# Half-empty products of a long convolution run in adjacent pairs, with channels turned modulo 8

## The chip, the cores and the metric

The kernel runs on one core of one Trainium2 chip. The metric is the device time of one execution in microseconds (us); less is better. A core has a matrix engine (TensorE, PE in the profile, with its weight loads as PEld), a vector engine (VectorE, DVE), a scalar engine (ScalarE, ACT), a general engine (GpSimd, POOL) and a queue engine (SyncE, SP), which here issues most of the transfers (DMAs). Matrix products read from the core's memory (SBUF, 128 partitions) and write to banks of a second memory (PSUM), from which DVE or ACT must take them away.

## The reference

One encoder layer over 2048 positions with 1024 channels. The input is normalised and projected; a part of the projection passes a width-3 convolution and then two rounds of a long two-sided convolution with gates (the Hyena group, 512 channels), the rest goes through a bidirectional mLSTM. Both are joined, projected and added to the input; cross-attention into 256 memory rows and an MLP follow, then a last normalisation. All is float32. What the change touches:

```python
def _hyena(hy, spec, skip):
    L = hy.shape[1]
    u = hy.astype(jnp.float32)
    z, g1, g2 = u[..., :D_HYENA], u[..., D_HYENA:2 * D_HYENA], u[..., 2 * D_HYENA:]
    for o, gate in enumerate((g1, g2)):
        conv = jnp.fft.irfft(jnp.fft.rfft(z, n=2 * L, axis=1) * spec[:, o], n=2 * L, axis=1)[:, :L]
        z = gate * (conv + z * skip[o].astype(jnp.float32))
    return z
```

`spec` is the spectrum of filters that a small network computes for every position: two sine layers of width 64, an output layer from 64 to 2 x 2 x 512 (two rounds, forward and backward filter), and a decay window.

## The kernel before, in words

The Fourier transforms of length 4096 are done as matrix products in two stages, with the sequence index written as t = 16 q + j (q from 0 to 127, j from 0 to 15). A first stage runs over q for each j: the matrix `f1`, two blocks of 128x128 for even and odd frequencies (`p`). It holds four copies of a 32-point transform, one for each value of q modulo 4; the rest of it is zeros. A second stage mixes j and q modulo 4 with one 128x128 block of `dm` per frequency. The way back has `em` for the second stage and `e2` (two blocks, summed) for the last. A tile of work is 128 partitions by 512 channels, one float32 product that fills one PSUM bank; the profile shows two records for it. The products of the projection and of later layers split their operands in high and low parts instead (`mm3`, lines 336 to 338, three products in a faster format).

The parts that the change touches:

- **`filters`** (205 to 322). For each of 8 steps j2, two rounds o and two j: the output layer gives the forward filter from rows 0 to 63 of the hidden layer (line 286, bank `pf`) and the backward filter from rows 64 to 127 (line 287, bank `pb`). Each is a product that uses 64 of the array's 128 rows. DVE multiplies both by the window (289, 290), DVE and GpSimd form sum and difference (294, 295), and `front` (268) applies `f1` (271), one iteration late. `blocks` (298) then loads the result by frequency and applies `dm` (319).
- **`sweep`** (652) projects 256 channels at a time, channels on partitions, and ends each column tile with the width-3 convolution. **`sweep_out`** (709) brings the tile into natural order: for the 12 tiles of the Hyena group it transposes 16 slices (time modulo 16, 63 or 65 positions each) on TensorE, four to a bank (719), copies each bank out on ACT or DVE in turn (721, `copy` at 171), and stores it with one DMA each (722).
- **`hyena`** (781). `spectrum` (851) applies `f1` to z: for each j two full products (856), copied out by ACT (p = 0) and DVE (p = 1) at 857 and stored at 859, one DMA on ACT's queue and one on SP's. Then 16 steps per round multiply by `dm` (880), by the filter's spectrum (882 to 886) and by `em` (846, in `back`). The last stage (891 to 902) sums two full products with `e2` in one bank (899), and DVE multiplies by the gate (900). In round one that is the next `spectrum`'s input, one iteration late. `load1`, `load2`, `load3` ask for data one or two steps ahead on SP's queue.

Order: `program` (1795) weaves `filters` with the first sweeps, then `hyena` with the remaining ones, by work units that the generators yield. A scheduler with a time model then fixes each engine's order of instructions, in which an engine waits at an instruction until all that it needs is there. PSUM has four banks for the projection (`mm`, 155) and four for the convolution (`hy`, 158), each used in turn. Products of the projection stand on TensorE between those of the convolution.

Of the kernel before, what the change touches and what calls it, by code (L numbers as in the profile page):

```python
# [18 lines left out]
L = 2048  # L19
# [8 lines left out]
def shape_constants():  # L28
# [30 lines left out]
    e2 = f1.transpose(0, 2, 1) * (wgt.reshape(2, 128, 1) / 4096.0)  # L59

# [8 lines left out]
    for par in range(2):  # L69
# [21 lines left out]
        "c_e2": e2.transpose(1, 0, 2),  # L91
# [34 lines left out]
class Prog:  # L126
    def __init__(self, ctx, tc, a):
        self.tc, self.nc, self.a = tc, tc.nc, a
        nc = self.nc
        self.ctx = ctx  # L130
        self.dr = ctx.enter_context(tc.tile_pool(name="dr", bufs=1, space=DRAM))
        self.s = {}
        cp = self.cp = ctx.enter_context(tc.tile_pool(name="cp", bufs=1))
        ident = cp.tile([128, 128], F32, name="ident")
        nc.gpsimd.memset(ident, 1.0)
        nc.gpsimd.affine_select(ident, ident, pattern=[[-1, 128]], compare_op=ALU.is_equal, fill=0.0,
                                base=0, channel_multiplier=1)
# [5 lines left out]
        self.flip = 0  # L143
        self.pending = []
# [13 lines left out]
    def hy(self):  # L158
        return self.ps.tile([128, 512], F32, tag="hy", name="hy", bufs=4)
# [45 lines left out]
    def filters(self):  # L205
# [4 lines left out]
        if True:  # L210
# [66 lines left out]
            for j2 in range(8):  # L277
# [3 lines left out]
                for o in range(2):  # L281
                    st = [ta() for p in range(2)]
                    for jj in range(2):
                        j = 2 * j2 + jj
                        pf, pb = self.hy(), self.hy()
                        nc.tensor.matmul(pf, hid[0:64, j], w3[0:64, o], start=True, stop=True)
                        nc.tensor.matmul(pb, hid[64:128, j], w3[64:128, o], start=True, stop=True)
# [421 lines left out]
    def sweep_out(self, ct, cv, t0, n):  # L709
# [3 lines left out]
        if ct < 12:  # L713
            q0, nq = t0 // 16, n // 16
            dst = self.d_hy[ct // 4].rearrange("(q j) c -> q j c", j=16)[q0:q0 + nq]
            for j4 in range(4):
                pt = self.mm().rearrange("p (k t) -> p k t", k=4)
                for jj in range(4):
                    nc.tensor.transpose(pt[0:nq, jj], cv[:, 4 * j4 + jj:n:16], self.ident)
                st = sb.tile([128, 4, 128], F32, tag="st", name="st", bufs=3)  # L720
                self.copy(st[0:nq], pt[0:nq])
                nc.sync.dma_start(out=dst[:, 4 * j4:4 * j4 + 4, cc], in_=st[0:nq])
            return
# [57 lines left out]
    def hyena(self, es):  # L781
        nc, tc, a = self.nc, self.tc, self.a
        hy = self.dram("hy", (3, L, CH)).rearrange("s (q j) c -> s q j c", j=16)
        hd = self.dram("hd", (2, 32, 128, CH))
        yh = self.dram("yh", (L, CH)).rearrange("(q j) c -> q j c", j=16)
        sds = [self.dram(f"zs{o}", (2, 128, 16, CH)) for o in range(2)]
        gds = [self.dram(f"zg{o}", (2, 128, 16, CH)) for o in range(2)]
# [8 lines left out]
        f1 = sb.tile([128, 2, 128], F32, name="f1")  # L796
        e2 = sb.tile([128, 2, 128], F32, name="e2")
        nc.sync.dma_start(out=f1, in_=a["c_f1"])
        nc.sync.dma_start(out=e2, in_=a["c_e2"])
        ghy = self.bcast(sb, a["hy_norm_g"], CH, "ghy")  # L800
        def load1(j2):
            z = ta()
            js = slice(2 * j2, 2 * j2 + 2)
            nc.sync.dma_start(out=z, in_=hy[0, :, js])
            return z

        def load2(o, i):
            p, k = divmod(2 * i, 16)
# [5 lines left out]
            nc.sync.dma_start(out=t, in_=sds[o][p, 8 * k:8 * k + 16].rearrange("(k r) j c -> (r j) k c", k=2))  # L814
# [29 lines left out]
        def back(m, em, y, gs, dst):  # L844
# [3 lines left out]
            if m == 1:  # L848
                nc.scalar.dma_start(out=dst.rearrange("(k r) j c -> (r j) k c", k=2), in_=gs)

        def spectrum(o, j2, z):
            st = [ta() for p in range(2)]
            for jj in range(2):
                for p in range(2):
                    pp = self.hy()
                    nc.tensor.matmul(pp, f1[:, p], z[:, jj], start=True, stop=True)
                    (nc.vector.tensor_copy if p else nc.scalar.copy)(st[p][:, jj], pp)
            for p in range(2):
                (nc.sync if p else nc.scalar).dma_start(out=sds[o][p, :, 2 * j2:2 * j2 + 2], in_=st[p])
# [7 lines left out]
        for o in range(2):  # L867
            gd = gds[o]
            nxt = load2(o, 0)
            for i in range(16):  # L870
                yield 3.5
                p, k = divmod(2 * i, 16)
# [5 lines left out]
                for m in range(2):  # L878
# [8 lines left out]
                    late(lambda m=m, em=em, y=y, gs=gs, dst=gd[p, 8 * k:8 * k + 16]: back(m, em, y, gs, dst))  # L887
            late(None)
            nxt = load3(o, 0)
            for j2 in range(8):  # L890
# [977 lines left out]
```

## Time and profile before

| | us |
|---|---|
| median of 3 runs | 3330.34 (3326.27 to 3330.63) |
| the profiled execution | 3330.7 |
| its span, first to last instruction | 3329.0 |
| TensorE busy in the span | 3162.2 |
| float32 products of lines 286 and 287, first to last start | 119.6 to 348.5 |
| first stages (line 856), first to last start | 497.4 to 848.8 |
| last stages (line 899), first to last start | 728.9 to 1144.5 |
| transposes of line 719, first to last start | 66.6 to 915.1 |

A row of the profile names line, engine, operation and tiles (`out<-in`), then count, busy time and the mean of one in ns. In rows of TensorE, 64*128 is rows by columns of the array that the product uses. A window row gives its length, then each engine's busy time with the number of instructions, the granted clock, the mean busy share of the 16 DMA engines, and GB/s. TensorE's instructions overlap, so the time that one costs is read from the starts, not from its duration.

### The profile page before, as it was taken

How to read it: one execution, taken by the hardware profiler on the slowest of the kernel's cores; microseconds unless marked ns; L12 is line 12 of the kernel's file. 1: busy time of each engine (PE TensorE's matmuls, PEld its weight loads, DVE VectorE, ACT ScalarE, POOL GpSimd, SP SyncE). 2: the span in 40 equal slices, each digit the busy share in tenths (PEclk: the TensorE clock that was granted, in tenths of full speed). 3: DMA queues.
4: the chain of work that ended last, by engine and by line, in shares of the span. 5: the costliest groups of instructions: out<-in, count | busy, mean ns of one | idle time of the engine just before them, and what ended most of it. 6: DMA issues, size and time to landing. Idle time of an engine off the chain costs nothing.

```text
span 3329.0 us, 45394 instructions
## 1 busy us (share of the span) xinstructions
PE 3162.2 (95%) x15293; PEld 2519.0 (76%) x15293; DVE 1985.2 (60%) x3334; ACT 1512.1 (45%) x2860; POOL 1253.5 (38%) x863
## 2 busy tenths in 40 slices
PE   6999999899999988699999998999999999999998
PEld 5655666667667887598888896888788887888876
DVE  7684324534556656576766564755755576656595
ACT  5442444642564344354454444555655543333335
POOL 0132000220122204634434114876765564434483
PEclk9999999999999999799999999999999999999999
DMA  5554897886787659857557525764754475444434
GB/s 177 177 195 135 284 316 244 241 262 237 217 225 251 211 182 310 262 155 246 172 179 238 191 89 175 229 216 155 222 172 144 161 240 169 127 143 138 130 93 167
DMA packets 472257, 655.70 MB, mean 197 GB/s; under 512 B 39630, under 2 KB 251854, under 8 KB 471000
## 3 DMA queue, kind: packets, MB, share of 16 engines
q1 hardware_dynamic: 436404, 594.23, 56.4%
q10 hardware_dynamic: 35620, 58.57, 4.8%
q8 instruction: 121, 1.98, 0.3%
q14 instruction: 112, 0.92, 0.1%
HBM read 437.67 MB, written 214.99 MB: 196 GB/s over the span
## 4 chain that ended last, share of the span: by engine, by line
PE 49%; DMA 4%; DVE 3%; issue 2%; POOL 1%; ACT 1%; SPq 0%; DVEq 0%; POOLq 0%; ACTq 0%
PE mm L338 10%; PE mm L336 10%; PE mm L337 10%; PE hy L338 5%; PE hy L336 5%; PE hy L337 5%; DMA rw<-rows 1%; DVE wl L341 1%; PE hy L1135 1%; DMA wr<-xs 1%; PE hy L1137 1%; PE hy L1370 0%; PE hy L1266 0%; DMA wn<-in_w_out_dram 0%; DMA wr<-in_ff_w_dram 0%
## 5 line engine op out<-in xcount | busy, mean ns | idle before, releaser
L341 DVE TENSOR_TENSOR wl<-wn,wh 128x512 fp32r<-128x512 f32 (+1 forms) x364 | 293.5, 841 | 124.3 <-ACT wh L341 111.4
L1449 DVE TENSOR_TENSOR bl<-wr,bh 128x512 fp32r<-128x512 f32 x213 | 239.0, 1128 | 130.5 <-ACT bh L1448 126.8
L1448 ACT CAST ah<-w 128x512 fp32r<-128x512 f32 x284 | 176.2, 622 | 301.0 <-PE hy L337 152.2
L885 POOL TENSOR_TENSOR b<-b,a 128x512 f32<-128x512 f32 x64 | 89.4, 1397 | 586.7 <-ACT b L883 351.1
L341 ACT CAST wh<-wn 128x512 fp32r<-128x512 f32 (+1 forms) x364 | 208.9, 618 | 198.3 <-PE mm L337 54.9
L336 PE MATMUL mm<-xh,wh 128*128 128x512 f32 x640 | 279.4, 438 | 6.6 <-ACT xh L496 2.7
L337 PE MATMUL mm<-xl,wh 128*128 128x512 f32 x640 | 276.8, 433 | 0.1
L338 PE MATMUL mm<-xh,wl 128*128 128x512 f32 x640 | 265.8, 416 | 0.0
L1449 DVE TENSOR_TENSOR al<-w,ah 128x512 fp32r<-128x512 f32 x236 | 219.1, 930 | 58.6 <-ACT ah L1448 58.3
L1448 ACT CAST bh<-wr 128x512 fp32r<-128x512 f32 x232 | 143.6, 621 | 235.7 <-PE mm L338 171.3
L338 PE MATMUL mm<-bh,al 128*128 128x512 f32 x576 | 225.5, 394 | 7.4 <-DVE al L1449 4.5
L336 PE MATMUL mm<-bh,ah 128*128 128x512 f32 x576 | 226.8, 394 | 0.1
L337 PE MATMUL mm<-bl,ah 128*128 128x512 f32 x576 | 225.8, 392 | 0.0
L336 PE MATMUL mm<-act,wh 128*128 128x512 f32 x512 | 200.1, 395 | 1.0 <-ACT wh L341 1.0
L337 PE MATMUL mm<-act,wh 128*128 128x512 f32 x512 | 200.7, 392 | 0.0
L338 PE MATMUL mm<-act,wl 128*128 128x512 f32 x512 | 199.1, 392 | 0.0
L1305 POOL TENSOR_TENSOR ssum<-ssum,sq 128x512 f32<-128x512 f32 x56 | 79.0, 1411 | 277.4 <-ACT sq L1304 274.3
L336 PE MATMUL hy<-bh,ah 128*128 128x512 f32 x448 | 175.2, 391 | 0.0
L337 PE MATMUL hy<-bl,ah 128*128 128x512 f32 x448 | 174.6, 390 | 0.0
L338 PE MATMUL hy<-bh,al 128*128 128x512 f32 x448 | 174.4, 390 | 0.0
L295 POOL TENSOR_TENSOR b<-b 128x512 f32<-128x512 f32 x32 | 66.5, 2079 | 284.6 <-DVE b L290 147.8
L336 PEld LDWEIGHTS mm<-xh,wh 128*128 128x128 f32 x640 | 122.2, 191 | 63.9 <-issue 29.1
(360 smaller groups left out, 8922.9 us busy)
## 6 DMA issues: line engine op xcount, KB each, us to landing
wr<-hc SPq DMA_DIRECT2D x224, 256.0 KB
w<-in_ff_w_dram SPq DMA_DIRECT2D x176, 256.0 KB
hc<-t SPq DMA_DIRECT2D x128, 256.0 KB
wn<-in_w_in_dram SPq DMA_DIRECT2D x100, 256.0 KB
hc<-q SPq DMA_DIRECT2D x96, 256.0 KB
fs<-a SPq DMA_DIRECT2D x32, 512.0 KB
a<-fs SPq DMA_DIRECT2D x32, 512.0 KB
hd<-a SPq DMA_DIRECT2D x32, 512.0 KB
```

Of the source, the lines that this page charges most:

```text
L295: nc.gpsimd.tensor_tensor(e[1], f, b, ALU.subtract)
L336: mm(ps, lh, rh, start=start, stop=False)
L337: mm(ps, lh, rl, start=False, stop=False)
L338: mm(ps, ll, rh, start=False, stop=stop)
L341: both = (self.nc.scalar.copy(hi, src), self.nc.vector.tensor_tensor(lo, src, hi.bitcast(F32), ALU.subtract))
L885: nc.gpsimd.tensor_tensor(xt, xt, hi[:, m], ALU.mult)
L1135: nc.tensor.matmul(dst, nm[:, h], va[:, h], start=True, stop=state is None)
L1137: nc.tensor.matmul(dst, rows_[d, 1][:, h], state[:, h], start=False, stop=True)
L1305: nc.gpsimd.tensor_tensor(ssum, ssum, sq, ALU.add)
L1448: self.nc.scalar.copy(hi, src)
L1449: eng.tensor_tensor(lo, src, hi.bitcast(F32), ALU.subtract)
```

## The change

A new method `beside` issues two products so that they follow each other directly on TensorE: the second-named one waits until the last readers of both banks are done, and the first-named one comes right behind it. It is used in three places.

- Output layer of the filters: the products of lines 286 and 287 become a pair.
- First stage in `hyena`: positions are loaded with the blocks of time outermost on the partitions (h = t // 512, 32 values of q for each h, `by_time`). With this order the matrix has an own 32x64 block for each h, the same four times. Two h fill 64 rows and 128 columns, even and odd frequencies together. So two full products become a pair, one on rows 0 to 63 and one on rows 64 to 127, each with a bank of its own.
- Last stage of round one: its two full products, summed in one bank, become a pair of which each gives 64 of the 128 columns, so the output is in the order by time that the next first stage wants. Round two keeps two full products in natural order.

The intermediate arrays in memory get the layout (32 frequencies, 2, 4 blocks of time, 16, 512). Loads by time come as four DMAs of 32 partitions, and the stages' loads and stores as two DMAs of 64 partitions in place of one of 128. `sweep_out` turns channels in 8 slices (time modulo 8, 126 or 128 positions each), and where 16 positions are left, in one more small transpose.

```diff
+    own = f1.reshape(2, 32, 4, 16, 2, 4)[:, :, 0, :, :, 0].transpose(1, 0, 2, 3).reshape(32, 64)
+    inv = e2.reshape(2, 16, 2, 4, 32, 4)[:, :, :, 0, :, 0].reshape(64, 32)
+    f1h = np.zeros((2, 2, 32, 2, 64))
+    e2h = np.zeros((2, 2, 2, 64, 128))
+    for h in range(4):
+        f1h[h // 2, h % 2, :, h % 2] = own
+        e2h[0, h // 2, h % 2, :, 32 * h:32 * h + 32] = inv
+        e2h[1, h // 2, h % 2, :, h::4] = inv
...
+    def beside(self, first, second):
+        n = self.banks.index(first[0].tensor.name)
+        held = self.banks[max(0, n - 4):max(0, n - 2)] if first[0].tensor.name != second[0].tensor.name else []
+        b = self.nc.tensor.matmul(*second, start=True, stop=True)
+        for i in reversed(self.nc.cur_bb.bb.instructions[-4000:]):
+            own = [x.bass_ap.tensor.name for x in i.ins if getattr(x, "bass_ap", None) is not None]
+            for t in [t for t in held if t in own]:
+                held.remove(t)
+                self.tc.add_manual_dep(b.ins, i.name, mybir.DependencyInfo(
+                    mybir.DependencyClass.Sync, mybir.DependencyReason.DATA), reason="beside")
+        with self.tc.high_priority(2000):
+            self.tc.keep_in_program_order(self.nc.tensor.matmul(*first, start=True, stop=True))
...
-                        nc.tensor.matmul(pf, hid[0:64, j], w3[0:64, o], start=True, stop=True)
-                        nc.tensor.matmul(pb, hid[64:128, j], w3[64:128, o], start=True, stop=True)
+                        self.beside((pf, hid[0:64, j], w3[0:64, o]), (pb, hid[64:128, j], w3[64:128, o]))
...
-            q0, nq = t0 // 16, n // 16
-            dst = self.d_hy[ct // 4].rearrange("(q j) c -> q j c", j=16)[q0:q0 + nq]
-            for j4 in range(4):
+            w = min(n // 8, 128)
+            dst = self.d_hy[ct // 4, t0:t0 + 8 * w, cc].rearrange("(q j) c -> q j c", j=8)
+            for j4 in range(2):
                 pt = self.mm().rearrange("p (k t) -> p k t", k=4)
                 for jj in range(4):
-                    nc.tensor.transpose(pt[0:nq, jj], cv[:, 4 * j4 + jj:n:16], self.ident)
+                    nc.tensor.transpose(pt[0:w, jj], cv[:, 4 * j4 + jj:8 * w:8], self.ident)
...
+            if n > 8 * w:
+                pt = self.mm()
+                nc.tensor.transpose(pt[0:16, 0:128], v[:, 8 * w:n], self.ident)
...
+        def by_time(t, s, js):
+            for h in range(4):
+                nc.sync.dma_start(out=t[32 * h:32 * h + 32], in_=hy[s, h, :, js])
+
+        def by_block(d, i):
+            return d[2 * i:2 * i + 2].rearrange("k r h j c -> (r h j) k c")
+
+        def by_pair(d, b, js):
+            v = d.rearrange("k r h j c -> h (k r) j c")
+            return [(slice(64 * g, 64 * g + 64), v[2 * b + g, :, js]) for g in range(2)]
...
-            for p in range(2):
-                nc.sync.dma_start(out=r[p], in_=gds[o][p, :, js])
+            for b in range(2):
+                for own, d in by_pair(gds[o], b, js):
+                    nc.sync.dma_start(out=r[b][own], in_=d)
             gate = ta()
-            nc.sync.dma_start(out=gate, in_=hy[1 + o, :, js])
+            if o:
+                nc.sync.dma_start(out=gate, in_=hq[2, :, js])
+            else:
+                by_time(gate, 1, js)
...
-                for p in range(2):
-                    pp = self.hy()
-                    nc.tensor.matmul(pp, f1[:, p], z[:, jj], start=True, stop=True)
-                    (nc.vector.tensor_copy if p else nc.scalar.copy)(st[p][:, jj], pp)
-            for p in range(2):
-                (nc.sync if p else nc.scalar).dma_start(out=sds[o][p, :, 2 * j2:2 * j2 + 2], in_=st[p])
+                pp = [self.hy() for b in range(2)]
+                self.beside(*((pp[b], f1[64 * b:64 * b + 64], z[64 * b:64 * b + 64, jj]) for b in range(2)))
+                for b in range(2):
+                    (nc.vector.tensor_copy if b else nc.scalar.copy)(st[b][:, jj], pp[b])
+            for b in range(2):
+                for own, d in by_pair(sds[o], b, slice(2 * j2, 2 * j2 + 2)):
+                    (nc.sync if b else nc.scalar).dma_start(out=d, in_=st[b][own])
...
-                    for p in range(2):
-                        nc.tensor.matmul(pp, e2[:, p], r[p][:, jj], start=p == 0, stop=p == 1)
+                    if o == 0:
+                        own = [slice(64 * b, 64 * b + 64) for b in range(2)]
+                        self.beside(*((pp[own[b]], e2[:, b, own[b]], r[b][:, jj]) for b in range(2)))
+                    else:
+                        for p in range(2):
+                            nc.tensor.matmul(pp, e2[:, 2 + p], r[p][:, jj], start=p == 0, stop=p == 1)
```

More of the change, by code (lines that the diff above doesn't have):

```diff
@@ L90, in shape_constants @@
         "c_f1": f1.transpose(1, 0, 2),
-        "c_e2": e2.transpose(1, 0, 2),
+        "c_f1h": f1h.reshape(128, 128),
+        "c_e2h": e2h.reshape(4, 128, 128).transpose(1, 0, 2),
         "c_dm": dm.transpose(1, 0, 2),
@@ L143, in __init__ @@
         self.flip = 0
+        self.banks = []
         self.pending = []
@@ L794, in tb @@
             return sb.tile([128, CH], F32, tag="b", name="b", bufs=5)
[L796 to L799, printed above, removed]
+        f1 = sb.tile([128, 128], F32, name="f1")
+        e2 = sb.tile([128, 4, 128], F32, name="e2")
+        nc.sync.dma_start(out=f1, in_=a["c_f1h"])
+        nc.sync.dma_start(out=e2, in_=a["c_e2h"])
         ghy = self.bcast(sb, a["hy_norm_g"], CH, "ghy")
@@ L803, in load1 @@
             js = slice(2 * j2, 2 * j2 + 2)
-            nc.sync.dma_start(out=z, in_=hy[0, :, js])
+            by_time(z, 0, js)
             return z
         def load2(o, i):
-            p, k = divmod(2 * i, 16)
             dm = sb.tile([128, 2, 128], F32, tag="dm", name="dm", bufs=2)
@@ L848, in back @@
             if m == 1:
-                nc.scalar.dma_start(out=dst.rearrange("(k r) j c -> (r j) k c", k=2), in_=gs)
+                nc.scalar.dma_start(out=dst, in_=gs)
         def spectrum(o, j2, z):
```

24 lines of the change are left out of this document (15 added, 9 removed).

## The prediction

> **What bounds the kernel now.** I read the page first, for where TensorE is full, then the windows of the part that the change touches, then what TensorE waits for there.
>
> ```profile
> span 3329.0 us, 45394 instructions
> PE 3162.2 (95%) x15293; PEld 2519.0 (76%) x15293; DVE 1985.2 (60%) x3334; ACT 1512.1 (45%) x2860; POOL 1253.5 (38%) x863
> ```
>
> ```profile
> core 0: us, PE busy (x) PEld busy (x) DVE busy (x) ACT busy (x) POOL busy (x), PEclk, DMA share, GB/s
> 100.00:360.00 260.00, 258.12 (x910) 150.22 (x909) 157.04 (x254) 94.93 (x155) 66.54 (x32) 0.99 0.49 162
> 360.00:490.00 130.00, 129.18 (x496) 86.35 (x495) 30.60 (x44) 60.97 (x103) 0.00 (x0) 1.00 0.95 328
> 490.00:560.00 70.00, 69.76 (x261) 46.98 (x261) 23.98 (x37) 24.85 (x38) 0.00 (x0) 1.00 0.75 259
> 560.00:740.00 180.00, 166.01 (x809) 122.00 (x808) 90.95 (x142) 110.27 (x178) 43.71 (x32) 0.98 0.80 239
> 740.00:850.00 110.00, 110.00 (x526) 76.92 (x526) 47.42 (x69) 30.90 (x52) 0.00 (x0) 1.00 0.68 240
> 850.00:1050.00 200.00, 191.93 (x778) 136.29 (x776) 117.83 (x168) 126.54 (x191) 47.62 (x33) 0.99 0.79 231
> ```
>
> The filters' output layer lies in 100 to 360 us, their spectrum blocks in 360 to 490, the first stage of round one in 490 to 560, and the last stage of round one with the first stage of round two in 740 to 850. In all four TensorE is busy 99% or more at a granted clock of 0.99 or 1.00, with the projection's products filling the gaps of the convolution. DVE is at 60% or less. DMA is the one other resource near its end, at 0.95 in 360 to 490. So TensorE time taken out of these windows comes off the span, as long as DMA can follow. What TensorE waits for from 100 to 1150 us is short (the two longest rows):
>
> ```profile
> PE hy L846 <- DVE b L886: 7.4, 7, 1.6
> PE mm L336 <- ACT st L174: 6.2, 3, 4.0
> ```
>
> **The price of each product.** Starts in the timeline of TensorE give it. A half-empty product alone (64 of 128 rows, two records in float32), then a pair that happens to be adjacent already, then full products:
>
> ```profile
> 156.79 1.12 PE L286 MATMUL hy<-fw,hid 64*128 64x512 f32 x2
> 157.84 0.50 PE L336 MATMUL mm<-xh,wh 128*128 128x512 f32 x1
> 158.18 0.40 PE L337 MATMUL mm<-xl,wh 128*128 128x512 f32 x1
> 158.42 0.40 PE L338 MATMUL mm<-xh,wl 128*128 128x512 f32 x1
> 158.75 1.12 PE L287 MATMUL hy<-fw,hid 64*128 64x512 f32 x2
> ```
>
> ```profile
> 199.84 0.71 PE L719 MATMUL mm<-ident,cv 128*63 128x128 f32 x5
> 200.48 0.69 PE L286 MATMUL hy<-fw,hid 64*128 64x512 f32 x1
> 200.49 0.69 PE L287 MATMUL hy<-fw,hid 64*128 64x512 f32 x1
> 201.01 0.59 PE L286 MATMUL hy<-fw,hid 64*128 64x512 f32 x1
> 201.02 0.59 PE L287 MATMUL hy<-fw,hid 64*128 64x512 f32 x1
> 201.54 0.59 PE L719 MATMUL mm<-ident,cv 128*63 128x128 f32 x3
> 201.89 0.48 PE L337 MATMUL mm<-xl,wh 128*128 128x512 f32 x1
> 202.20 0.40 PE L338 MATMUL mm<-xh,wl 128*128 128x512 f32 x1
> ```
>
> ```profile
> 500.87 1.36 PE L719 MATMUL mm<-ident,cv 128*63 128x128 f32 x11
> 501.99 0.48 PE L336 MATMUL mm<-xh,wh 128*128 128x512 f32 x1
> 502.30 0.40 PE L337 MATMUL mm<-xl,wh 128*128 128x512 f32 x1
> 502.54 0.40 PE L338 MATMUL mm<-xh,wl 128*128 128x512 f32 x1
> 502.77 0.39 PE L336 MATMUL mm<-xh,wh 128*128 128x512 f32 x1
> 503.00 2.74 PE L856 MATMUL hy<-a,f 128*128 128x512 f32 x6
> 505.17 0.79 PE L337 MATMUL mm<-xl,wh 128*128 128x512 f32 x1
> 505.80 0.40 PE L338 MATMUL mm<-xh,wl 128*128 128x512 f32 x1
> ```
>
> A projection product steps by 0.23 to 0.24 (502.30 to 503.00 is three). Alone, a half-empty product costs 158.75 - 156.79 - 3 x 0.235 = 1.25 us. Three full products (six records) and one projection product take 505.80 - 503.00 = 2.80, so a full one costs (2.80 - 0.23) / 3 = 0.86. A half-empty product thus costs 0.39 *more* than a full one: going into and out of the split array is paid for. Eleven transposes and one projection product take 502.30 - 500.87 = 1.43, so a transpose costs (1.43 - 0.235) / 11 = 0.11. The pair: 202.20 - 199.84 = 2.36, less eight transposes (0.88) and one projection product (0.235), is 1.25. Its four records start two and two, 0.01 us apart. So **a pair side by side costs what one half costs, 1.25**, and a second pair directly behind it should cost 0.86, as it pays no second entry.
>
> The Trainium skill (TensorEngine Tiling (Array Packing), Key Properties) says that changing the tiling mode drains TensorE. The 0.39 us agrees for row halves; the 63-column transposes, which the program marks as 128x64 tiles, show no such step. By that rule each of the 31 stretches of row pairs in the first stages, where today nothing is split, pays an entry; that is already in the 1.25.
>
> **The change, part by part.**
>
> ```profile
> L286 PE MATMUL hy<-fw,hid x64: 589/589/693, 119.6 to 346.4; 64*128 64x512 f32 x64
> L856 PE MATMUL hy<-a,f x128: 590/592/595, 497.4 to 848.8; 128*128 128x512 f32 x128
> L719 PE MATMUL mm<-ident,cv x384: 270/273/379, 66.6 to 915.1; 128*63 128x128 f32 x96, 128*65 128x128 f32 x96
> ```
>
> These rows of the lines' own view say when each runs and how often (records; a float32 product has two, a transpose one). How products stand next to each other comes from the two programs' orders of instructions.
>
> (a) *Filters' output layer.* Today 46 of its 64 halves stand alone, seven pairs are adjacent by themselves, and one stretch has two pairs: 46 x 1.25 + 7 x 1.25 + 2.11 = 68.4 us. Afterwards all 32 pairs are adjacent, in 31 stretches: 30 x 1.25 + 2.11 = 39.6. Gain **28.8**.
>
> (b) *First stages of both rounds.* 64 full products become 32 row pairs of the form that (a) shows, again 31 stretches: 64 x 0.86 = 55.0 against 39.6. Gain **15.4**, half of it in 490 to 560, half in 740 to 850.
>
> (c) *Last stage of round one.* 32 full products (27.5 us) become 16 pairs that split the array by columns, mostly two pairs in a row: eight stretches. No trace row shows such a pair. If the split is free, as the 63-column transposes suggest, it costs 16 x 0.86 = 13.8, gain 13.7; if the two halves run one after the other with an entry per stretch, 8 x (0.39 + 4 x 0.86) = 30.6, a loss of 3.1. The nearest row for two products in a split array is the row pair: 8 x (1.25 + 0.86) = 16.9, gain **10.6**. I take that.
>
> (d) *Channels turned modulo 8.* 384 transposes become 192 with 126 or 128 columns and 12 of 16. The time of one follows the 128 columns of the identity that stream by, the same in both forms of the row above. 180 fewer at 0.11 give **19.8**. Evacuations fall from 96 to 60; DVE and ACT are not full, so that is worth nothing by itself.
>
> (e) *More, smaller transfers.* Loads by time come in four pieces, the stages' loads and stores in halves. SP issues 60 more DMAs (2060 become 2120) and ACT 16 more; bytes stay.
>
> ```profile
> L859 SPq DMA_DIRECT2D zs<-a x16: 319/320/1694, 502.3 to 850.2; - x16
> L859 ACTq DMA_DIRECT2D zs<-a x16: 326/326/360, 502.4 to 849.0; - x16
> ```
>
> At about 0.33 us each that is 20 us of SP's queue and 5 of ACT's, over some 800 us. Cost nothing: ACT is under 65% busy in each window, and loads are asked for one step ahead; without that cover a step's last piece lands some 1 us later, 16 steps of it. The skill (DMA: Bandwidth & Descriptors, Rules for kernel authors) advises one 128-partition transfer in place of two halves, as halves share the same engines; the halves here would save nothing by themselves, and no row prices them against each other.
>
> (f) *A wait.* The first-issued product of a pair waits until both PSUM banks are free, where each half waited for its own. Behind it on TensorE stands all else, the projection too, and ACT's copies of the projection wait for that. Cost taken: nothing, as these lines never waited for a bank. The price if not is a rival.
>
> (a) to (d) sum to 74.6. Against it I set what will not shrink with TensorE: with the pairs, the order of instructions packs the last stage of round one and the next first stage between 222 of the projection's products where 458 stood, so loads must come faster. TensorE idles 14 of 180 us (8%) in 560 to 740, where DMA is at 0.80; 8% of the some 90 us that 740 to 850 becomes is **7**. Net 67.6. The profiled execution took 3330.7 us, 1.7 beyond its span; the median of the three is 3330.34. 3330.3 - 67.6 = **3263**.
>
> **The rivals.**
>
> *DMA or its latency sets the packed stages.* For: 0.95 in 360 to 490. Against: TensorE is still 99% busy there. The transposes of that window:
>
> ```profile
> 360.00:490.00 130.00, 12.05 (x88) 11.95 (x89) 1.00 0.95 328
> ```
>
> Then (c), half of (b) and the gain on these transposes (88 of 384, 4.5 us) are lost: 10.6 + 7.7 + 4.5 - 7 already charged = 16 more: 3279.
>
> *Column halves do not overlap* (the change does not do there what it says). 13.7 worse: 3277. The Trainium skill (TensorE: Matmul & The Clock Gate, Measured speedup vs the span model) reports 2.38 times for three column tiles; by it the halves would overlap, and no run here shows it.
>
> *Waiting for both banks stalls TensorE: slower than before.* A bank is freed by DVE:
>
> ```profile
> L289 DVE TENSOR_TENSOR b<-hy,a 128x512 f32<-128x512 f32 x32 | 22.0, 688 | 50.3 <-PE hy L286 47.1 <-issue 2.0 <-PE hy L287 1.1
> L290 DVE TENSOR_TENSOR b<-hy,a 128x512 f32<-128x512 f32 x32 | 21.9, 686 | 16.7 <-PE hy L287 16.7
> ```
>
> If each of the 80 pairs waited for two such readers, 2 x 0.69 = 1.4, that is 110 us: 3373. It decides from 67.6 / 80 = 0.85 us a pair. Against: DVE waits for TensorE there, not the reverse, and projection products stand between nearly all pairs.
>
> *More than forecast.* The column split is free (3.1), nothing is charged (7) and half of the 14 us idle in 560 to 740 is filled, as more of the projection now stands there (7): 3246.
>
> **How the numbers follow.** Forecast 0.58, DMA 0.17, column halves 0.10, stall 0.10, more 0.05. The range takes in the unknown of (c) on both sides, and DMA together with serial column halves, 3292, with a few us for what the new order of all else costs: **3243 to 3300**. It leaves out the stall and little else. About 0.2% (6.7 us) is what a measurement can tell from no change. All cases but the stall are faster by more; of the stall's 0.10 I put 0.07 slower, 0.02 within and 0.01 faster: faster 0.91, same 0.02, slower 0.07.
>
> **What would show it.** In the timeline after, both records of a pair should start within 0.02 us and a pair take 1.25. Column pairs starting 0.86 apart would make (c) wrong. The transposes should show 204 records. The windows should stay at 99% TensorE; a DMA share near 1 with idle TensorE makes the 7 us too small. Rows of TensorE waiting for DVE or ACT at the pairs' lines would make (f) wrong. The work behind the convolution should take the same time, only start some 68 us sooner; if it does not, the sum of windows before 1050 us is not what sets the end.

## The result, and the profile after

| | before | after |
|---|---|---|
| median of 4 runs, us | 3330.49 (3326.27 to 3331.05) | 3292.78 (3282.89 to 3293.89) |
| ratio | | 0.988, 95% interval 0.9863 to 0.9896 |
| the profiled execution / its span, us | 3330.7 / 3329.0 | 3292.63 / 3290.9 |

The change is faster by 37.7 us by the medians (40 by the ratio), inside the range, but little more than half of the 67.6 that were forecast. One thing in the text on the change has to be put right: h is (t // 16) mod 4, the remainder of q by 4, and not t // 512, so the "blocks of time" are the four sets of q with equal remainder. No price hangs on it.

The head of the page after:

```profile
span 3290.9 us, 45063 instructions
PE 3097.7 (94%) x15113; PEld 2470.2 (75%) x15113; DVE 1971.7 (60%) x3316; ACT 1502.7 (46%) x2842; POOL 1242.2 (38%) x863
```

TensorE is busy 64.5 us less (3162.2 - 3097.7), most of the 74.6 of work that were forecast, yet the span shrinks by 38.1. So TensorE waits more. The windows of the changed part show where (length, busy time and number of instructions of each engine, granted clock, DMA share, GB/s):

```profile
350.00:475.00 125.00, 125.00 (x451) 81.91 (x450) 23.69 (x36) 60.54 (x99) 0.00 (x0) 1.00 0.94 326
475.00:545.00 70.00, 64.98 (x261) 41.11 (x260) 27.00 (x42) 26.50 (x41) 0.00 (x0) 1.00 0.89 248
545.00:705.00 160.00, 146.39 (x783) 108.68 (x782) 79.01 (x124) 99.70 (x164) 41.97 (x32) 1.00 0.85 255
705.00:730.00 25.00, 23.32 (x155) 17.11 (x153) 5.07 (x8) 4.27 (x10) 0.00 (x0) 1.00 1.02 258
730.00:760.00 30.00, 24.12 (x125) 14.77 (x126) 14.23 (x23) 7.15 (x14) 0.00 (x0) 0.94 0.98 277
760.00:790.00 30.00, 26.07 (x110) 14.96 (x110) 14.29 (x22) 8.80 (x15) 0.00 (x0) 0.94 0.99 280
790.00:815.00 25.00, 21.01 (x76) 11.95 (x73) 13.17 (x17) 6.96 (x10) 0.00 (x0) 0.86 0.66 193
```

The packed stage (last stage of round one with the first stage of round two) now lies in 705 to 815. Before, TensorE was busy there all the time at a DMA share of 0.68; now it idles 15.5 of 110 us, the DMA share is near 1 up to 790 us, and the granted clock sinks to 0.94 and 0.86. The first stage of round one (475 to 545) idles 5 us at a share of 0.89 where it idled 0.2 at 0.75.

The timeline of TensorE in the packed stage shows the pairs themselves, first two column pairs and then, after a stretch of projection products, a row pair (a product has two records):

```profile
724.63 0.28 PE L361 MATMUL mm<-wh,xh 128*128 128x256 f32 x1
724.85 0.64 PE L177 MATMUL hy<-a,e 128*64 128x512 f32 x1
724.85 0.64 PE L185 MATMUL hy<-a,e 128*64 128x512 f32 x1
725.33 0.59 PE L177 MATMUL hy<-a,e 128*64 128x512 f32 x1
725.33 0.59 PE L185 MATMUL hy<-a,e 128*64 128x512 f32 x1
725.75 0.59 PE L177 MATMUL hy<-a,e 128*64 128x512 f32 x1
725.76 0.59 PE L185 MATMUL hy<-a,e 128*64 128x512 f32 x1
726.18 0.59 PE L177 MATMUL hy<-a,e 128*64 128x512 f32 x1
726.19 0.59 PE L185 MATMUL hy<-a,e 128*64 128x512 f32 x1
726.71 0.39 PE L362 MATMUL mm<-wl,xh 128*128 128x256 f32 x1
726.94 0.28 PE L363 MATMUL mm<-wh,xl 128*128 128x256 f32 x1
...
728.37 0.28 PE L363 MATMUL mm<-wh,xl 128*128 128x256 f32 x1
731.44 0.67 PE L177 MATMUL hy<-a,f 64*128 64x512 f32 x1 [2.79 <-ACT st L804]
731.45 0.69 PE L185 MATMUL hy<-a,f 64*128 64x512 f32 x1
731.95 0.59 PE L177 MATMUL hy<-a,f 64*128 64x512 f32 x1
731.98 0.59 PE L185 MATMUL hy<-a,f 64*128 64x512 f32 x1
732.50 0.39 PE L361 MATMUL mm<-wh,xh 128*128 128x256 f32 x1
```

The halves shown here start within 0.03 us of each other, by rows and by columns. In the whole trace 140 of the 160 pairs of records start within 0.02 us, the other 20 lie 0.04 to 0.13 us apart, still well inside the 0.59 us of a record. Two column pairs take 726.71 - 724.85 = 1.86 us from their first start to the next product's. The prediction reckons otherwise: it takes in what is lost before and behind a pair. By its way they take 726.94 - 724.63 = 2.31, less two projection products of 0.12 each (twelve of them run from 726.94 to 728.37), so 2.07. The pairs do what they were said to do. In front of the row pair TensorE stands still for 2.79 us.

What TensorE waited for from 700 to 816 us, where the same view of the kernel before has no row at all for 738 to 851 (the five longest rows; total us, times, longest):

```profile
PE hy L177 <- ACT a L903: 4.1, 3, 3.1
PE mm L361 <- ACT xh L366: 3.3, 1, 3.3
PE hy L177 <- ACT st L804: 2.8, 1, 2.8
PE hy L177 <- DMA a<-zg: 2.3, 2, 1.9
PE hy L177 <- DVE a L903: 2.1, 1, 2.1
```

Some name a load that had not come (`DMA a<-zg`), some the copy of a bank (`a L903`), some a copy for the projection. ACT and DVE wait for loads in turn: from 690 to 830 us ACT waits 15.6 us for weights of the projection (`wn`) and DVE 15.2 for its input (`xt`).

**A ruler for the experiments.** The convolution ends with its last stage: the products of line 899 start last at 1144.5 before, and those after at 1108.1. What lies behind hardly changes: 3329.0 - 1145.1 = 2183.9 us before, 3290.9 - 1108.7 = 2182.2 after, and 2177 to 2189 in all kernels of the table below. So the stretch from 100 us to the end of the convolution is where the time is made, and one window row of it gives TensorE's work and its idle time. Before, with a row of the packed stage, then the same two of after:

```profile
100.00:1145.10 1045.10, 1015.36 (x4346) 694.84 (x4344) 531.74 (x863) 474.60 (x770) 185.58 (x115) 0.99 0.71 230
...
705.00:790.00 85.00, 83.32 (x459) 61.17 (x459) 25.75 (x38) 26.30 (x50) 6.39 (x5) 1.00 0.76 266
```

```profile
100.00:1108.70 1008.70, 952.10 (x4178) 648.84 (x4178) 515.62 (x835) 463.93 (x750) 174.93 (x115) 0.98 0.78 238
...
705.00:790.00 85.00, 73.51 (x388) 46.84 (x388) 33.59 (x53) 20.22 (x37) 0.00 (x0) 0.96 1.00 273
```

Work fell by 63.3 us, idle time rose from 29.7 to 56.6, by 26.9: 36.4 net, of the 38.1 by which the span shrinks. The second pair of rows holds a hint: 0.76 of the DMA engines' time moved 266 GB/s before, and all of it moves 273 after. The same bytes cost 0.286 of share per 100 GB/s before and 0.366 after, 28% more. The transfers that the change cuts up come in packets of 4 KB: by the packet records of the traces these took 176 ns on average in this window before and 236 after.

### The profile page after: what moved, and what is told of

It reads as the page before. It is cut to its first block, busy times and chain, and to the rows that moved or that the text cites. A ratio compares the mean times of both kernels' runs of the same rounds, so it can differ in the third digit from the quotient of the medians.

```text
span 3290.9 us, 45063 instructions
## 1 busy us (share of the span) xinstructions
PE 3097.7 (94%) x15113; PEld 2470.2 (75%) x15113; DVE 1971.7 (60%) x3316; ACT 1502.7 (46%) x2842; POOL 1242.2 (38%) x863
## 4 chain that ended last, share of the span: by engine, by line
PE 66%; DMA 14%; DVE 8%; issue 5%; ACT 3%; POOL 2%; SPq 1%; ACTq 0%; DVEq 0%; POOLq 0%
PE mm L361 14%; PE mm L363 13%; PE mm L362 13%; PE hy L363 5%; PE hy L361 5%; PE hy L362 5%; DVE wl L366 2%; PE hy L344 2%; DMA rw<-rows 2%; PE hy L297 2%; DMA wn<-in_w_in_dram 1%; DMA a<-zg 1%; DMA a<-hd 1%; PE hy L177 1%; PE hy L892 1%
## 5 line engine op out<-in xcount | busy, mean ns | idle before, releaser
L366 DVE TENSOR_TENSOR wl<-wn,wh 128x512 fp32r<-128x512 f32 (+1 forms) x364 | 285.9, 820 | 147.8 <-ACT wh L366 144.0
L362 PE MATMUL mm<-xl,wh 128*128 128x512 f32 x640 | 270.2, 423 | 2.2 <-DVE xl L366 1.6
L1499 DVE TENSOR_TENSOR al<-w,ah 128x512 fp32r<-128x512 f32 x236 | 226.0, 959 | 61.4 <-ACT ah L1498 61.1
L362 PEld LDWEIGHTS mm<-xl,wh 128*128 128x128 f32 x640 | 122.7, 192 | 53.8 <-issue 26.2
```

The source lines that it names most:

```text
L362: mm(ps, lh, rl, start=False, stop=False)
L366: both = (self.nc.scalar.copy(hi, src), self.nc.vector.tensor_tensor(lo, src, hi.bitcast(F32), ALU.subtract))
L1499: eng.tensor_tensor(lo, src, hi.bitcast(F32), ALU.subtract)
```

## The experiments

**Theory.** The prices of the work are right; the transfers of 32 and 64 partitions are slower per byte, and in the packed stage, which asks for more bytes per microsecond, they run out. **Rival, packing:** too little of the projection stands between the pairs of the packed stage, whatever the transfers. **Rival, prices:** a term of (a) to (d) doesn't earn what it should.

All ratios are to the kernel before on the same chip; the stretch is that of the ruler. Each stretch is of one execution, and executions of one kernel differ by 10 us (those of the filters' pairs alone: 3293.95, the one profiled, to 3304.44), so a difference of a few us between two stretches shows nothing by itself.

| kernel | ratio | interval | end of stretch | busy | idle |
|---|---|---|---|---|---|
| before | 1 | | 1145.1 | 1015.4 | 29.7 |
| after | 0.988 | 0.9863 to 0.9896 | 1108.7 | 952.1 | 56.6 |
| filters' pairs alone | 0.9924 | 0.9907 to 0.994 | 1113.3 | 985.8 | 27.5 |
| turned channels alone | 0.9909 | 0.9892 to 0.9925 | 1126.5 | 993.3 | 33.2 |
| both of these | 0.9867 | 0.9846 to 0.9889 | 1106.1 | 967.8 | 38.3 |
| all but these two | 0.9985 | 0.9974 to 0.9996 | 1143.1 | 997.8 | 45.3 |
| before, narrow transfers | 0.9991 | 0.9977 to 1.0005 | 1147.8 | 1015.4 | 32.4 |
| after, whole transfers | 0.9814 | 0.9796 to 0.9831 | 1088.9 | 940.1 | 48.8 |
| after, loads by time whole | 0.9868 | 0.9851 to 0.9884 | 1103.6 | 949.9 | 53.7 |
| after, halves whole | 0.985 | 0.9835 to 0.9865 | 1096.1 | 944.9 | 51.2 |

**1. The parts.** Filters' pairs alone: the kernel before, with line 286 to 287 replaced.

```diff
-                        nc.tensor.matmul(pf, hid[0:64, j], w3[0:64, o], start=True, stop=True)
-                        nc.tensor.matmul(pb, hid[64:128, j], w3[64:128, o], start=True, stop=True)
+                        self.beside((pf, hid[0:64, j], w3[0:64, o]), (pb, hid[64:128, j], w3[64:128, o]))
```

> The kernel before with the pairs of the filters' output layer alone. Price 28.8 us; of the 7.6 us of new idle time that the two parts together showed up to the 800th product, 5 stand in one wait at the end of the filters. If the prices hold part by part: 22 to 29 us faster, ratio 0.9913 to 0.9934, and the other 15 to 22 of the 44 are the transposes' (priced 19.8). If pairs stall on their banks: under 15 us, ratio above 0.9955.

```profile
100.00:1113.30 1013.30, 985.82 (x4346) 686.89 (x4345) 535.50 (x864) 474.95 (x770) 181.01 (x115) 0.99 0.74 238
```

The work falls by 29.5 (1015.4 - 985.8), 28.8 were forecast; the time falls by 0.76% (0.60 to 0.93), 25 us (20 to 31).

Turned channels alone: the kernel before with `sweep_out` of after (the diff of `sweep_out` above, nothing else).

> The kernel before with nothing but the channels turned modulo 8 inside a chunk, so that a group's transposes are four of [64, 128] onto one side where eight stood; the filters, the loads and stores and all products are those of before. If the four parts add up, this earns what lies between the filters alone (0.9924) and the filters with the turn (0.9867): some 19 us, ratio 0.994, against 19.8 us forecast. If the turn earns only beside the paired filters, or the 5-us wait at the filters' end comes from it, the ratio is above 0.996.

```profile
100.00:1126.50 1026.50, 993.26 (x4172) 671.21 (x4171) 519.68 (x846) 463.35 (x750) 175.47 (x115) 0.99 0.72 234
```

The work falls by 22.1 and the convolution ends 18.6 sooner, for 19.8 forecast. The time falls by 30 us (25 to 36), more than the 19 expected: here some 7 us more come from behind the convolution (3303.5 - 1126.5 = 2177.0 in place of 2183.9), which no step foresaw.

Both, that is (a) and (d) without the convolution's own changes:

> The kernel before with only the pairs of the filters' output layer and the channels turned modulo 8; the convolution's stages, their layout and their transfers stay as before. Prices of (a) and (d): 28.8 + 19.8 = 48.6 us. Theory N (narrow transfers: DMAs that touch only 32 or 64 partitions move the same packets more slowly, and the convolution's stages starve TensorE): none of them is here, so 40 to 49 us faster than before, that is 3282 to 3290, as fast as the whole change or faster. Theory P (packing: the new order of instructions asks for the same transfers in a shorter stage): the same, 3282 to 3290. Theory B (a pair's wait for both PSUM banks stalls TensorE): these pairs wait too, at the 0.3 us a pair that the whole change lost on average, so some 10 us less gain: 3292 or more.

```profile
100.00:1106.10 1006.10, 967.75 (x4173) 668.48 (x4172) 517.66 (x844) 464.55 (x751) 175.74 (x115) 0.98 0.74 239
```

The work falls by 47.6 (forecast 48.6). But idle time rises by 8.6. The waits of TensorE in that stretch hold one that is long by itself, a transpose that waits for DVE at the end of the filters:

```profile
PE mm L735 <- DVE P L696: 4.8, 1, 4.8
```

That wait is also in the whole change. So the two don't add up in full, and together they already earn 44 us (37 to 51): **as much as the whole change**, 40 (35 to 46).

The other half, the whole change with the old output layer and the old `sweep_out`:

> The other half of the change: pairs, layout and narrow transfers of the convolution's stages, without the filters' pairs and with channels turned modulo 16 as before. Prices of (b) and (c): 26 us; of the 31 us of new idle time some 24 fell in these stages. Theories N and P: 0 to 8 us faster than before, 3322 to 3330. Theory B: about 80 pairs shared 31 us of waits, 48 of them are here: 26 - 19, so 7 faster, 3323; this run does not part B from the others, but with the first it tells which part of the change earns the gain.

```profile
100.00:1143.10 1043.10, 997.80 (x4345) 674.23 (x4344) 532.95 (x869) 473.14 (x770) 183.40 (x115) 0.98 0.75 231
```

Of 26.0 forecast for (b) and (c), 5 us arrive (1 to 9). The work falls by 17.6, and idle time rises by 15.6. So the loss lies in the convolution's part.

**2. The transfers.** First the narrow transfers by themselves, in the kernel before, whose order of rows stays as it is:

```diff
-            nc.sync.dma_start(out=z, in_=hy[0, :, js])
+            for h in range(4):
+                nc.sync.dma_start(out=z[32 * h:32 * h + 32], in_=hy[0, 32 * h:32 * h + 32, js])
...
-                nc.sync.dma_start(out=r[p], in_=gds[o][p, :, js])
+                for g in range(2):
+                    nc.sync.dma_start(out=r[p][64 * g:64 * g + 64], in_=gds[o][p, 64 * g:64 * g + 64, js])
```

and in the same way the gate of round one in quarters, and the stores of `spectrum` in halves.

> The kernel before, with all its products, and only its transfers cut: loads by time in four pieces of 32 partitions, the first and last stages' loads and stores in two of 64. Theory N: TensorE's work is unchanged, the 4 KB packets take longer than the 159 ns (median) of before, and the stages that were just fed are no longer: 10 to 30 us slower, 3340 to 3360. Theories P and B: within 5 us of before, packets as before.

```profile
705.00:790.00 85.00, 83.41 (x447) 60.07 (x446) 26.06 (x39) 26.01 (x49) 6.83 (x6) 1.00 0.89 262
```

No loss that can be measured: the 10 to 30 us of theory N did not come. But the row shows the price: 0.89 of the DMA engines' time for 262 GB/s, 0.340 per 100 GB/s in place of 0.286, and 224 ns for a packet of 4 KB in place of 176. The stage without pairs has DMA time to spare, so TensorE stays at 98%. This alone would have spoken for the forecast's "cost nothing"; it needs its counterpart.

That is the whole change with every transfer on 128 partitions. Rows then lie in a wrong order on the partitions; the permutation is left out, the bytes and the work are the same.

```diff
-            for h in range(4):
-                nc.sync.dma_start(out=t[32 * h:32 * h + 32], in_=hy[s, h, :, js])
+            nc.sync.dma_start(out=t, in_=hq[s, :, js])
...
-            v = d.rearrange("k r h j c -> h (k r) j c")
-            return [(slice(64 * g, 64 * g + 64), v[2 * b + g, :, js]) for g in range(2)]
+            v = d.rearrange("k r h j c -> (k r h) j c")
+            return [(slice(0, 128), v[128 * b:128 * b + 128, js])]
```

> The changed kernel with all its pairs, but every transfer of the convolution covers 128 partitions in one DMA; the rows then land in a wrong order, so the permutation of the data is left out, and the numbers in the output with it. Theory N: TensorE is fed again, 4 KB packets are back at about 160 ns, and the time falls to 3263 to 3275. Theory P: same bytes in the same packed stage, 3288 to 3295. Theory B: the waits stay, 3288 to 3295.

```profile
100.00:1088.90 988.90, 940.05 (x4171) 641.66 (x4170) 519.30 (x846) 464.69 (x751) 175.79 (x115) 0.99 0.76 243
...
705.00:790.00 85.00, 81.72 (x417) 50.54 (x414) 47.33 (x71) 27.02 (x45) 0.00 (x0) 1.00 0.87 305
```

The gain is 62 us (56 to 68) in place of 40, and the convolution ends 19.8 us sooner than in the change. **The work falls by 75.3; 74.6 was forecast.** The packed stage takes 305 GB/s at a share of 0.87, which is 0.285 per 100 GB/s, the price of before, and a packet of 4 KB takes 179 ns. At the price of the narrow transfers 305 GB/s would need a share of 1.12. That settles the theory against the rival of the prices: the DMA engines, loaded by the narrow transfers, hold the packed stage back. ACT's wait for `wn` falls from 15.6 to 7.3 us and DVE's for `xt` from 15.2 to 9.2. It also bounds the rival of packing: the stage holds 275 of the projection's products for 259 in the change, so it is packed nearly as closely, and yet TensorE idles 3.3 of these 85 us in place of 11.5.

The edit alters one thing more: the rows of a transfer lie 32 KB apart in memory, as before, in place of 128. Two kernels speak against that as the cause. In the kernel before with narrow transfers the rows stayed 32 KB apart, and the packets became dear; in the nested kernel below they lie 128 KB apart, and its packets of 4 KB took 160 ns from 600 to 690 us, though at a DMA share of only 0.16.

Which of them? One half of that edit at a time; each leaves the permutation out for its own rows. Only the loads by time whole:

> The changed kernel, with the loads by time as one DMA of 128 partitions (the rows land in a wrong order: that permutation is left out); the first and last stages' halves stay. All transfers whole gave about 18 us over the whole change (ratio 0.981 against 0.988 of before). If what costs is the bytes that go through narrow transfers, the loads by time are 0.5 of 2.5 MB a step in the packed stage: about 4 us faster than the whole change, ratio 0.987. If it is the 32 partitions alone, that is quarters and not halves, nearly all 18: ratio 0.982.

```profile
705.00:790.00 85.00, 73.93 (x387) 46.02 (x386) 38.05 (x58) 22.63 (x40) 0.00 (x0) 0.96 0.97 275
```

Only the halves of the stages whole:

> The changed kernel, with the first and last stages' loads and stores as one DMA of 128 partitions (rows in a wrong order: that permutation is left out); the loads by time stay in quarters. If the cost goes by narrow bytes: about 14 of the 18 us, ratio 0.984. If the quarters alone cost: as the whole change, 0.988.

```profile
705.00:790.00 85.00, 79.38 (x408) 49.29 (x408) 44.27 (x67) 25.61 (x44) 0.00 (x0) 0.96 0.89 292
```

The convolution ends 5.1 and 12.6 us sooner than in the change, and 0.353 and 0.305 of share go into 100 GB/s. By bytes the loads by time are 2 of 10 tiles (z and one gate, against two stores and two loads in each round); by the number of pieces added they are 48 of 112 (43%). They earn 5.1 of 17.7, 29%, between the two, but one execution each doesn't tell one rule from the other: the ratio with the loads by time whole, 0.9868, is not told apart from the change's 0.988. Only the case that the quarters alone cost, with nearly all 18 us for them, falls. The two do not quite add up to the 19.8 of both, by less than executions differ.

**3. Remedies.** If the narrow transfers lose because one queue issues their pieces one after the other, the second half of each can go to ACT's queue:

```diff
-                nc.sync.dma_start(out=t[32 * h:32 * h + 32], in_=hy[s, h, :, js])
+                (nc.scalar if h // 2 else nc.sync).dma_start(out=t[32 * h:32 * h + 32], in_=hy[s, h, :, js])
...
-                    nc.sync.dma_start(out=r[b][own], in_=d)
+                    (nc.scalar if g else nc.sync).dma_start(out=r[b][own], in_=d)
...
-                    (nc.sync if b else nc.scalar).dma_start(out=d, in_=st[b][own])
+                    (nc.scalar if g else nc.sync).dma_start(out=d, in_=st[b][own])
```

> The whole change, outputs complete, with the second half of each narrow load and store issued on ACT's queue and the first on SP's, so that the two halves of the partitions are in flight together. Theory ports (the 4 KB packets take 236 ns in place of 175 because all engines work on the same half of the partitions at a time): packets come back to 160 to 190 ns, the last stage of round two ends near where it does with whole transfers, ratio 0.981 to 0.985. If a narrow transfer is slow whatever runs beside it: packets stay at 225 or more, ratio 0.986 to 0.990. If ACT's copies wait behind the loads that ACT now issues (16 steps, some us each): above 0.990.

The packed stage:

```profile
705.00:790.00 85.00, 72.90 (x371) 46.90 (x370) 31.95 (x50) 18.68 (x35) 0.00 (x0) 0.89 0.97 268
```

Two rows of ACT's waits from 700 to 815 us, each ended by a load:

```profile
ACT st L802 <- DMA a<-hy: 17.7, 1, 17.7
ACT xh L366 <- DMA a<-hy: 13.5, 2, 8.9
```

0.9899 (0.9882 to 0.9917), not told apart from the change. The price stays at 0.362 per 100 GB/s and a packet of 4 KB at 236 ns, so it isn't SP's queue that makes it. And ACT, which now issues loads, waits with its copies behind them.

The pieces can also be one DMA with a nested side in memory (`hy[s, :, :, js]`, and `v[2 * b:2 * b + 2, :, js]` onto all 128 partitions):

> The whole change, outputs complete, with each set of pieces as one DMA of 128 partitions whose side in memory is nested: two blocks of 64 rows, or four of 32. If a DMA is spread over all 16 engines as the plain ones are, this is as good as whole transfers in a wrong order: ratio 0.980 to 0.984. If the outermost count of 2 or 4 decides how many engines take part, 64 packets of 4 KB at 0.16 us stand one after another on an engine, 10 us a DMA and four DMAs a step in the packed stage: over 100 us slower than before. The Trainium skill (DMA: Bandwidth & Descriptors, Why a DMA increments its semaphore by 16 and not by 1) states the second as a rule.

```profile
600.00:690.00 90.00, 30.63 (x114) 19.45 (x112) 11.73 (x17) 10.30 (x15) 0.00 (x0) 0.65 0.16 66
```

1.1624 (1.1599 to 1.1649), some 540 us slower than before. In the first stage the DMA engines are busy 0.16 of the time on average, at 66 GB/s, and TensorE idles two thirds. The Trainium skill (DMA: Bandwidth & Descriptors, Why a DMA increments its semaphore by 16 and not by 1) says that a transfer is spread over the largest number of engines, up to 16, that divides the slowest dimension of both sides; here that is 4 or 2. The row agrees: 2 or 4 of 16 are 0.125 or 0.25, and the share of 0.16 lies between.

A layout of its own that keeps the first and last stage's transfers whole and cuts the second stage's loads and stores, and the loads by time, into two halves each:

```diff
-        sds = [self.dram(f"zs{o}", (32, 2, 4, 16, CH)) for o in range(2)]
+        sds = [self.dram(f"zs{o}", (2, 32, 2, 2, 16, CH)) for o in range(2)]
...
+            return [(slice(64 * b, 64 * b + 64), d[b, 2 * i:2 * i + 2].rearrange("k g r j c -> (g r j) k c")) for b in range(2)]
...
+            return [(slice(0, 128), d[b].rearrange("k g r j c -> (k g r) j c")[:, js])]
```

(with the constants permuted to suit).

> The changed kernel with another layout of the intermediate arrays, outputs complete: first and last stages load and store 128 partitions in one DMA, loads by time come as two halves, and the second stage, which has about 160 us for its 16 steps, loads and stores in halves instead. Theory narrow and packed together: the packed stage is fed, 10 to 18 us faster than the whole change, ratio 0.983 to 0.985. If narrow transfers cost wherever they stand: the loss only moves, ratio 0.987 to 0.990.

Against packing: more of the projection between the steps of the packed stage, by the work units that its step yields.

```diff
-                yield 3.5 if o else 7.0
+                yield 3.5 if o else 10.5
```

> The changed kernel with one number altered: the last stage of round one yields 10.5 work units a step in place of 7, so that more of the projection is placed in it: its last stage and the next first stage lie between 414 of the projection's products in place of 259. Theory packing: transfers have more time and the 20 to 27 us of idle TensorE in this stage mostly go, 10 to 20 us faster than the whole change, ratio 0.982 to 0.985, if the steps behind do not miss the products moved. Narrow transfers as the sole cause, at whatever spacing: 0 to 4 us, ratio 0.987 to 0.988.

The last products of the convolution and of the projection, first of after, then of the layout, then of the spread kernel:

```profile
L949 PE MATMUL hy<-a,e x64: 590/592/1222, 1014.6 to 1108.1; 128*128 128x512 f32 x64
L361 PE MATMUL mm<-wh,xh x512: 276/283/1215, 577.6 to 1201.2; 128*128 128x256 f32 x128, 128*128 128x272 f32 x43
```

```profile
L952 PE MATMUL hy<-a,e x64: 591/592/593, 1026.8 to 1126.5; 128*128 128x512 f32 x64
L363 PE MATMUL mm<-wh,xh x512: 274/283/691, 579.7 to 1184.4; 128*128 128x256 f32 x128, 128*128 128x272 f32 x43
```

```profile
L949 PE MATMUL hy<-a,e x64: 591/592/592, 1053.3 to 1156.1; 128*128 128x512 f32 x64
L361 PE MATMUL mm<-wh,xh x512: 277/283/1215, 575.5 to 1191.6; 128*128 128x256 f32 x128, 128*128 128x272 f32 x43
```

The layout measured 0.9926 (0.991 to 0.9942), the spread kernel 1.0001 (0.999 to 1.0011). Both finish the projection *sooner* than the change, by 17 and 10 us, and are yet slower by 15 and 40 us. Their convolution ends later, by 18 and 48 us. So my expectation for both was wrong, in the same way: I had counted TensorE's work done by some moment, and the span follows the end of the convolution. Projection products that fill its gaps put it off: from 100 us to its end TensorE runs 4426 records in the layout and 4548 in the spread kernel, for 4178 in the change. They are not paid back in full behind it (3329.8 - 1156.7 = 2173.1 in the spread kernel, only 9 us less than after). The remedy against packing fails, and the idle time of the stretch doesn't fall with it (61.0 us in the spread kernel for 56.6). Whether an earlier end alone would help wasn't measured: two more kernels, the layout and the change with another weight between convolution and projection (280 for 227), gave no result.

## Why the prediction was right in sign and too large

**(a) to (d), the prices: right.** With whole transfers the work fell by 75.3 for 74.6. (a) alone gave 29.5 of work for 28.8, (d) alone 22.1 for 19.8. (c) was right in kind: two column pairs take 2.07 us, between the free split (1.72) and the row pair that I took (2.11); 27.5 - 8 x 2.07 = 10.9 for 10.6 forecast. The rival of column halves that don't overlap falls.

**(e) "Cost nothing": this is the step that failed**, and with it the 7 us of idle time charged beside it. I priced the transfers by their issue, with bytes that "stay". The bytes stayed and each became dearer:

```profile
L906 SPq DMA_DIRECT2D zs<-a x32: 445/467/2250, 490.0 to 813.0; - x32
L874 SPq DMA_DIRECT2D a<-zg x64: 444/548/1948, 704.0 to 1083.0; - x64
```

Even the issue of a half took 0.45 us at least, for 0.32 of the whole one. What decided is the share: 0.366 per 100 GB/s for 0.286. The DMA share of 0.68 that I read as room in 740 to 850 would have been 0.87 at the new price and the old pace, and the pairs quickened the pace. The 7 us were taken from a window with a share of 0.80; the two kernels with narrow and whole transfers put 19.8 us on the difference. The 222 products of the projection that I set in the packed stage are 259 in the trace, so it was packed less closely than I took.

Part of it isn't idle time but a slower clock. From 705 to 850 us in after and then in the kernel with whole transfers:

```profile
705.00:850.00 145.00, 126.25 (x580) 81.49 (x579) 67.59 (x99) 48.29 (x79) 5.63 (x5) 0.93 0.90 248
```

```profile
705.00:850.00 145.00, 132.85 (x614) 86.12 (x611) 83.53 (x122) 60.89 (x98) 13.22 (x9) 0.99 0.83 269
```

0.06 of clock over 145 us is an estimate of 8.7 us (7.6 over the 126 in which TensorE is busy), most of the 12.0 by which the work differs (952.1 - 940.1). The clock was lower where the waits stood, 0.94 and 0.86 in the rows from 730 to 815 us; that the waits lower it was not tried. If they do, a wait was paid twice in the change: as itself, and in the clock around it.

**(f) The wait for both banks "cost nothing": nearly.** Pairs waited for the copies of their banks. For ACT's this is the row of the whole stretch up to the convolution's end, and for DVE's the 2.1 us shown above are all:

```profile
PE hy L177 <- ACT a L903: 7.6, 5, 3.1
```

That is about 10 us, against 110 of the rival that stalls at every pair. With whole transfers the same copies held the pairs back twice, for 2.7 us in all. So most of it came with the narrow transfers; that it is theirs alone wasn't tried.

**The DMA rival** ("DMA or its latency sets the packed stages", 3279) was right in kind and had a chance of 0.17. It took the loss from TensorE's terms and capped it at 16 us; the narrow transfers cost 20. That the time came out at the 3292 up to which the range was argued is luck: that figure needs column halves that don't overlap, and they do.

**What is left.** Even with whole transfers 19.1 us of new idle time stand in the stretch, for 7 charged; 8.6 came with (a) and (d) alone, one wait of 4.8 us among them. The rest is hardly in the packed stage, where the 7 were charged. By the rows above TensorE idles 3.3 us from 705 to 790, but 12.2 from 705 to 850: 8.9 us lie behind the last pair (786.4 us), in the second stage of round two. What makes these stays open. **What the text was to show:** 204 transposes came as said (192 + 12), and 140 of 160 pairs of records started within 0.02 us; the windows did not stay at 99%, a DMA share near 1 with idle TensorE did appear, and the work behind the convolution took the same time (2183.9 and 2182.2).

## What to carry to other kernels

When a layout cuts transfers into pieces that touch fewer partitions, price the bytes again: compare DMA share per GB/s, not the share alone, and multiply it by the pace that the faster kernel will ask for. Before work is moved to fill gaps, look for the point that sets the end (here the last product of the convolution), and count what the fillers put in front of it. Parts of a change that don't touch the layout can hold all its gain: here two of them alone are as fast as the whole.

## What the runs showed that was not expected

With transfers of 32 and 64 partitions a byte took 19% more DMA time in the kernel before (0.340 to 0.286) and 26 to 28% more in the change, on two issuing queues or one; whole transfers of the same window are in these figures. Why wasn't found; which engine or port they crowd can't be read from these views. No kernel here has both the order by time and plain whole transfers in all stages, so the 62 us measure what the narrow transfers cost and are not a version of this change.
